# Rows of score maxima by VectorE's 32x32 transposition in place of a TensorE product

## The chip, the cores and the metric

One core of a Trainium2 chip. The metric is the device time of one execution in microseconds (us), taken as the median over runs. Engines: TensorE (PE, with its weight loads as PEld), VectorE (DVE), ScalarE (ACT), GpSimd (POOL) and SyncE (SP), whose queue issues nearly all DMAs here.

## What is computed

Two layers over 2048 tokens of width 1024: a Mamba-2 layer, then a multi-head latent attention. The change lies in the attention, whose core in the reference is

```python
for i in range(S // Q_BLOCK):                  # blocks of 128 queries
    s = einsum('bqhd,bkhd->bhqk', q_nope, k_nope[:, :kv_len]) + \
        einsum('bqhr,bkr->bhqk', q_rope, k_rope[:, :kv_len])
    s = s * scale
    p = softmax(where(mask, s, -inf), axis=-1)
    outs.append(einsum('bhqk,bkhd->bqhd', p, v[:, :kv_len]))
```

with 16 heads, queries and keys of 64 + 32 channels and values of 64. The softmax needs for each query something near its largest score, so that the exponentials stay in range.

## The kernel before

The program runs the Mamba layer and the projections first, then `heads` (the attention), then `back` (gate, output projection, final norm). Only `heads` is touched.

`heads` works on 64 *jobs*, one for each head h (0 to 15) and block qb (0 to 3) of 512 queries. A job has 4 qb + 4 *units*, one for each block kb of 128 keys; the last four are on the causal diagonal. There are 640 units in all, and as many *chunks* of the first pass.

- **First pass, `maxima`** (one chunk of it per step): a product of 128 queries by up to 512 keys in the high half of the fp16 pairs (L1235, on the diagonal with a mask product L1237) into a PSUM tile, and VectorE's maximum over the keys (L1238) into one column of `mx`. After a job's last chunk VectorE makes of `mx` (through `m` and `me`) the 128x8 numbers `nm`: for each of the 128 queries of the job's four groups the negative maximum divided by 64, as an fp16 value (columns 0 to 3, L1249) and its remainder (4 to 7, L1250).
- **`row`**: the numbers of a job must become two rows of 512 queries, since they enter the scores as two more channels: rows 96 and 97 of the query tile `quer[h, qb]`, against constant rows of 64 in the keys. TensorE multiplies `nm` (as weights, 128x128 and zero beyond column 8) by the identity `idb` (L1255), VectorE copies the 8x128 result from PSUM into `rT` (L1257), and SP writes `rT` to DRAM (`m_d`, L1258) and reads it back as 2x512 (L1259). The read waits for the write.
- **Second pass, `scores`** for unit i: three products of 128 keys by 512 queries (L1269 to L1271, the first with 98 channels, that is with the row; L1273 adds the mask on the diagonal), ScalarE's exponential from PSUM (L1275, `x`) and its fp16 copy (L1277, `PTs`), then the remainder `x` - `PTs` by VectorE or, for two in five units off the diagonal, by GpSimd (L1279).
- **`values`**, three units behind: two products for each of up to four query groups (L1291, L1293) into "tr" tiles, and at the end of a half job `finish` (`Ot`, `ri`, `Oa`, `Op`); `store` turns the results of a pair of heads.

TensorE's order is the order in which the code is written (a manual schedule for that engine); on the others the scheduler sets the order. One step of the loop emits at most one or two chunks of maxima, then what is due in `later` (rows, stores), then the scores of unit i, then the values of unit i - 3. All maxima of a job must be out `READY` = 7 units ahead of its first unit; the job's row follows `ROWS` = 2 steps after its last chunk. Where small jobs follow large ones the chunks run further ahead, so a row of qb = 3 is made about 5 units before it is used, rows of the others earlier. Maxima, rows, scores and stores take their PSUM tiles in turn from the four of tag "mm"; a tile is free again when its reader has read it. `rT` and `nm` have two tiles each.

Of the kernel before, what the change touches and what calls it, by code (L numbers as in the profile page):

```python
# [13 lines left out]
F16 = mybir.dt.float16  # L14
# [7 lines left out]
P = 128  # L22
# [5 lines left out]
NH = 16  # L28
EPS = 1e-6
TB = 512  # L30
NB = T // TB
# [8 lines left out]
EV1 = ['big', 'yT', 'Xp', 'big', 'Sp']  # L40
HELD = 3
READY = 7
ROWS = 2
TURN = 4
MSCALE = 64.0
LN16 = 2.772588722239781
# [21 lines left out]
class Net:  # L68
# [716 lines left out]
    def ssd(self, b, g):  # L785
# [30 lines left out]
        for c in range(4):  # L816
# [9 lines left out]
            def between():  # L826
                pi = self.t(self.pp, "tr", [P, TB], bufs=4)
                self.mm3(pi, Ct[:, 0], Ct[:, 1], old[:, 0], old[:, 1], True, True)
                t = self.t(self.sp, "yt", [P, TB], bufs=2)
                v.tensor_tensor(v8(t), v8(pi), heads(ecum), ALU.mult)  # L830
                return t
# [23 lines left out]
            with self.tc.high_priority(20):  # L855
                v.tensor_tensor(v8(Xd), v8(px), heads(dt), ALU.mult)
# [335 lines left out]
    def heads(self, sp):  # L1192
        nc, v, act, mm = self.nc, self.nc.vector, self.nc.scalar.activation, self.nc.tensor.matmul
        keys, vals, quer = self.keys, self.vals, self.quer
        turned = [self.t(sp, f"nm{i}", [P, P], F16, bufs=1) for i in range(2)]
        for u in turned:
            nc.gpsimd.memset(u, 0.0)

# [11 lines left out]
        jobs = [(h, qb) for h in range(NH) for qb in range(NB)]  # L1210
        chunks, ends = [], []
# [14 lines left out]
        def maxima(n, j, i, c0, w, last):  # L1226

            h, qb = jobs[n]
            if (j, i) == (0, 0):
                peak[n] = self.t(sp, "mx", [P, 4, 4], bufs=3)  # L1230
                if n + 2 < len(jobs):
                    self.load_q(*jobs[n + 2])
            Q, K, qs = quer[h, qb], keys[h % 2], slice(j * P, (j + 1) * P)
            s = self.t(self.pp, "mm", [P, TB], bufs=4)
            mm(s[:, :w], Q[0:96, 0, qs], K[0:96, 0, c0:c0 + w], start=True, stop=not last)  # L1235
            if last:
                mm(s[:, w - P:w], self.idb, self.mk, start=False, stop=True)  # L1237
            v.tensor_reduce(peak[n][:, j, i:i + 1], s[:, :w], AX.X, ALU.max)  # L1238
            if last and j == 3:
                m = peak.pop(n)  # L1240
                if qb:
                    x = self.t(sp, "m", [P, 4], bufs=2)
                    v.tensor_reduce(x, m[:, :, :qb + 1], AX.X, ALU.max)
                else:
                    x = m[:, :, 0]
                e = self.t(sp, "me", [P, 4], bufs=2)
                v.tensor_scalar(e, x, -1.0 / MSCALE, LN16 / MSCALE, ALU.mult, ALU.add)
                u = turned[n % 2]
                v.tensor_copy(u[:, 0:4], e)  # L1249
                v.tensor_tensor(u[:, 4:8], e, u[:, 0:4], ALU.subtract)  # L1250

        def row(n):

            ps = self.t(self.pp, "mm", [P, TB], bufs=4)
            mm(ps[:, 0:P], turned[n % 2], self.idb, start=True, stop=True)  # L1255
            r = self.t(sp, "rT", [8, P], F16, bufs=2)
            v.tensor_copy(r, ps[0:8, 0:P])  # L1257
            nc.sync.dma_start(self.m_d[n], r)  # L1258
            nc.sync.dma_start(quer[jobs[n]][96:98, 0, :], self.m_d[n].rearrange("(s j) q -> s (j q)", s=2))  # L1259

        def scores(i):

            n, kb = units[i]
            h, qb = jobs[n]
            jj = max(kb - 4 * qb, 0)
            diag = kb >= 4 * qb
            Q, K, ks, c = quer[h, qb], keys[h % 2], slice(kb * P, (kb + 1) * P), slice(jj * P, TB)
            s = self.t(self.pp, "mm", [P, TB], bufs=4)
            mm(s[:, c], K[0:98, 0, ks], Q[0:98, 0, c], start=True, stop=False)  # L1269
            mm(s[:, c], K[0:96, 0, ks], Q[0:96, 1, c], start=False, stop=False)  # L1270
            mm(s[:, c], K[0:96, 1, ks], Q[0:96, 0, c], start=False, stop=not diag)  # L1271
            if diag:
                mm(s[:, jj * P:(jj + 1) * P], self.mk, self.idb, start=False, stop=True)  # L1273
            x = self.t(sp, "x", [P, TB], bufs=4)
            act(x[:, c], s[:, c], AF.Exp)  # L1275
            u = self.t(sp, "PTs", [P, 2, TB], F16, bufs=HELD + 2)
            act(u[:, 0, c], x[:, c], AF.Copy)  # L1277
            engine = nc.gpsimd if not diag and i % 5 in (1, 3) else v
            engine.tensor_tensor(u[:, 1, c], x[:, c], u[:, 0, c], ALU.subtract)  # L1279
            return u  # L1280

        def values(i, u):

            n, kb = units[i]
            h, qb = jobs[n]
            V = vals[h % 2]
            if kb == 0:
                outs[n] = [self.t(self.pp, "tr", [P, 2, 256], bufs=4) for _ in range(2)]
            for j in range(max(kb - 4 * qb, 0), 4):
                o, js = outs[n][j // 2][:, j % 2], slice(j * P, (j + 1) * P)  # L1290
                mm(o[:, 0:130], u[:, 0, js], V[:, kb, :], start=kb == 0 and j % 2 == 0, stop=False,  # L1291
                   skip_group_check=True)
                mm(o[:, 64:130], u[:, 1, js], V[:, kb, 64:130], start=False, stop=kb == 4 * qb + j,  # L1293
                   skip_group_check=True)
            if kb in (4 * qb + 1, 4 * qb + 3):
                finish(n, (kb - 4 * qb) // 2)
            if kb == 4 * NB - 1 and h + 2 < NH:
                self.load_k(h + 2, 0, NB)
                self.load_v(h + 2)
# [32 lines left out]
        step, later, held, made = [0], [], [], 0  # L1332
# [3 lines left out]
        def waiting():  # L1336
            for at, f in list(later):
                if at <= step[0]:
                    later.remove((at, f))
                    f()  # L1340

        for i in range(len(units)):
            step[0] = i
            while made < due[i]:
                maxima(*chunks[made])
                made += 1
                n = chunks[made - 1][0]
                if made == ends[n]:
                    if i:
                        later.append((i + ROWS, lambda n=n: row(n)))  # L1350
                    else:
                        row(n)
            waiting()
            held.append((i, scores(i)))
            if len(held) > HELD:
                values(*held.pop(0))
# [121 lines left out]
    def run(self):  # L1478
        tc = self.tc
        with ExitStack() as whole:  # L1480
            cp = whole.enter_context(tc.tile_pool(name="const", bufs=1))
            dp = whole.enter_context(tc.tile_pool(name="dram", bufs=1, space=DRAM))
            self.pp = whole.enter_context(tc.tile_pool(name="pp", bufs=4, space=PSUM))
            self.sm = whole.enter_context(tc.tile_pool(name="sm", bufs=4))
            self.constants(cp)
            self.h_d = dp.tile([T, D], F32, name="h_d")
            self.gate_d = dp.tile([D, T], F32, name="gate_d")
            self.o_d = dp.tile([D, T], F32, name="o_d")
            self.m_d = dp.tile([NH * NB, 8, P], F16, name="m_d")
            self.qn_d = dp.tile([1024, 2, T], F16, name="qn_d")  # L1490
            self.q1_d = dp.tile([256, 2, T], F16, name="q1_d")
            self.q2_d = dp.tile([256, 2, T], F16, name="q2_d")
            self.kn_d = dp.tile([1024, 2, T], F16, name="kn_d")
            self.kr_d = dp.tile([32, 2, T], F16, name="kr_d")
            self.v_d = dp.tile([T, 2048], F16, name="v_d")
            self.wd_d = dp.tile([KD, P, 2, 288], F16, name="wd_d")
            self.wq_d = dp.tile([KD, P, 2, 384], F16, name="wq_d")
            self.wg_d = [dp.tile([KD, P, 2, TB], F16, name=f"wg{n}_d") for n in range(2)]
            self.wu_d = [dp.tile([2 if n < 4 else 3, P, 2, TB], F16, name=f"wu{n}_d") for n in range(7)]
            self.us_d = dp.tile([1024], F32, name="us_d")  # L1500
            self.wi_d = [dp.tile([G, KD // 2, P, 2, 2, n], F16, name=f"wi{i}_d") for i, n in enumerate((256, 512, 512))]
            self.wo_d = dp.tile([G, 2, 2, P, 2, 2, TB], F16, name="wo_d")
            self.xq = whole.enter_context(tc.tile_pool(name="xq", bufs=8, side="right"))
            self.layers()
            self.attention()
            self.back()
            self.tail.close()
# [50 lines left out]
```

## Time and profile before

| | |
|---|---|
| median of 3 runs | 3020.39 us (3019.53 to 3021.72) |
| profiled execution | 3012.66 us |
| its span, first to last instruction | 3010.9 us |
| busy in the span | PE 2871.6 us (95%), DVE 2281.5 (76%), ACT 1885.9 (63%), POOL 665.7 (22%) |
| the attention | about 2000 to 2815 us of the span |

The shares are averages over stages: ahead of the attention TensorE alone is full, in the attention TensorE, VectorE and ScalarE are all well used. In the lists, a line reads: time or total, engine, source line, operation, what it writes <- what it reads; a bracket behind an instruction gives how long its engine stood idle before it and what released it. The numbers of matrix products' ends are modelled, so consecutive ones overlap in the list.

### The profile page before, as it was taken

What the parts mean: (1) busy time and instruction counts of PE and PEld (TensorE: products, weight loads), DVE (VectorE), ACT (ScalarE), POOL (GpSimd) and SP (SyncE); (2) the same over time, 40 slices, a digit from 0 to 9 for tenths busy, and PEclk for the clock granted to TensorE, in tenths of its full rate; (3) what the DMA queues carried; (4) which work ended last, traced back from release to release, by engine and by line L of the source; (5) the groups of instructions that cost most, each with busy time, mean ns of one, the idle gap of its engine ahead of it and who ended that gap; (6) DMA issues with size and microseconds to landing.
All of it is one profiled execution on the core that took longest, in us unless ns stands there. A gap on an engine that the chain in (4) does not pass through costs nothing.

```text
span 3010.9 us, 55172 instructions
## 1 busy us (share of the span) xinstructions
PE 2871.6 (95%) x19726; PEld 1686.8 (56%) x19726; DVE 2281.5 (76%) x5162; ACT 1885.9 (63%) x4360; POOL 665.7 (22%) x798
## 2 busy tenths in 40 slices
PE   7899999999999999999999999989999999998998
PEld 3456656555555554544555454545666656665787
DVE  6789987787877788787855544368988989898554
ACT  8777666665766666565543433338888888887622
POOL 0212122121222112221111212113232323234200
PEclk9999999999999999999999999999999999999999
DMA  8765435544464456455357555631212121222462
GB/s 284 241 227 179 155 116 196 175 154 141 168 212 157 145 175 198 172 165 186 123 162 262 176 167 194 201 96 43 62 43 69 43 62 43 69 64 74 141 210 105
DMA packets 234248, 440.70 MB, mean 146 GB/s; under 512 B 59218, under 2 KB 101010, under 8 KB 232532
## 3 DMA queue, kind: packets, MB, share of 16 engines
q1 hardware_dynamic: 222836, 401.24, 41.9%
q0 software_dynamic: 11136, 35.92, 3.3%
q8 instruction: 155, 2.54, 0.3%
q14 instruction: 121, 0.99, 0.1%
HBM read 332.73 MB, written 104.34 MB: 145 GB/s over the span
## 4 chain that ended last, share of the span: by engine, by line
PE 60%; DVE 19%; ACT 10%; issue 6%; DMA 4%; POOL 1%; SPq 0%; ACTq 0%; DVEq 0%; POOLq 0%
PE mm L84 11%; PE mm L86 11%; PE mm L85 11%; PE tr L85 4%; PE tr L84 4%; PE tr L86 4%; DVE cacc L612 4%; ACT x L1275 3%; DVE PTs L1279 3%; DVE mx L1238 3%; ACT PTs L1277 2%; PE mm L1269 2%; PE mm L1270 2%; PE mm L1271 2%; PE tr L1291 2%
## 5 line engine op out<-in xcount | busy, mean ns | idle before, releaser
L1275 ACT ACTIVATE x<-mm 128x512 f32<-128x512 f32 (+3 forms) x640 | 336.1, 525 | 124.9 <-PE mm L1271 59.2
L1238 DVE TENSOR_REDUCE mx<-mm 128x1 f32<-128x512 f32 (+3 forms) x640 | 378.4, 602 | 39.3 <-PE mm L1237 23.4
L1277 ACT ACTIVATE PTs<-x 128x512 f16<-128x512 f32 (+3 forms) x640 | 361.7, 566 | 16.2
L1279 DVE TENSOR_TENSOR PTs<-x,PTs 128x512 f16<-128x512 f32 (+3 forms) x512 | 306.9, 604 | 45.3 <-ACT PTs L1277 35.2
L84 PE MATMUL mm<-xT,wsp 128*128 128x512 f16 x800 | 306.7, 383 | 6.3 <-ACT wsp L115 4.2
L85 PE MATMUL mm<-xT,wsp 128*128 128x512 f16 x800 | 305.7, 382 | 0.0
L86 PE MATMUL mm<-xT,wsp 128*128 128x512 f16 x800 | 305.3, 382 | 0.0
L1291 PE MATMUL tr<-K,PTs 128*128 128x130 f16 x2176 | 280.0, 222 | 0.0
L1293 PE MATMUL tr<-K,PTs 128*128 128x66 f16 x2176 | 260.5, 194 | 9.0 <-POOL PTs L1279 6.2
L1291 PEld LDWEIGHTS <-PTs 128*128 128x128 f16 x2176 | 203.8, 98 | 61.4 <-issue 4.5
L84 PE MATMUL mm<-wsp,xT 128*128 128x512 f16 (+1 forms) x640 | 230.3, 361 | 4.7 <-ACT craw L606 4.5
L85 PE MATMUL mm<-wsp,xT 128*128 128x512 f16 (+1 forms) x640 | 230.5, 360 | 3.2 <-DVE wsp L116 3.2
L612 DVE SCALAR_TENSOR_TENSOR cacc<-craw,pack,cacc 128x512 f32<-128x512 f32 x288 | 214.1, 771 | 24.2 <-ACT cacc L610 23.2
L1269 PE MATMUL mm<-xT,K 98*128 98x512 f16 (+3 forms) x640 | 227.2, 355 | 4.3 <-DVE mx L1238 3.4
L1293 PEld LDWEIGHTS <-PTs 128*128 128x128 f16 x2176 | 197.7, 98 | 59.7 <-POOL PTs L1279 7.9
L86 PE MATMUL mm<-wsp,xT 128*128 128x512 f16 (+1 forms) x640 | 230.5, 360 | 0.0
L1270 PE MATMUL mm<-xT,K 96*128 96x512 f16 (+3 forms) x640 | 227.1, 355 | 0.0
L1235 PE MATMUL mm<-K,xT 96*128 96x512 f16 (+3 forms) x640 | 225.2, 358 | 1.1 <-DVE Xp L116 1.1
L1271 PE MATMUL mm<-xT,K 96*128 96x512 f16 (+3 forms) x640 | 225.6, 352 | 0.0
L802 POOL TENSOR_TENSOR Xp<-Xw,Xp 128x512 fp32r<-128x512 f32 x64 | 89.6, 1400 | 499.6 <-ACT Xp L801 280.5
L84 PE MATMUL mm<-wsp,yT 128*128 128x512 f16 (+1 forms) x512 | 197.5, 386 | 2.2 <-DVE sz L636 1.6
L86 PE MATMUL mm<-wsp,yT 128*128 128x512 f16 (+1 forms) x512 | 195.8, 382 | 0.0
(461 smaller groups left out, 6946.9 us busy)
## 6 DMA issues: line engine op xcount, KB each, us to landing
wsp<-wi_d SPq DMA_DIRECT2D x96, 512.0 KB
big<-cumT SPq DMA_DIRECT2D x64, 512.0 KB
wraw<-in_ssm_w_out_dram SPq DMA_DIRECT2D x96, 256.0 KB
wi_d<-wsp SPq DMA_DIRECT2D x32, 512.0 KB
wsp<-wo_d SPq DMA_DIRECT2D x32, 512.0 KB
wsp<-wu_d SPq DMA_DIRECT2D x28, 512.0 KB
hx<-in_ssm_w_in_dram SPq DMA_DIRECT2D x48, 256.0 KB
wraw<-in_ssm_w_in_dram SPq DMA_DIRECT2D x48, 256.0 KB
```

The costliest lines, as they stand in the source:

```text
L84: mm(out, l_hi, r_hi, start=start, stop=False)
L85: mm(out, l_hi, r_lo, start=False, stop=False)
L86: mm(out, l_lo, r_hi, start=False, stop=stop)
L612: nc.vector.scalar_tensor_tensor(acc, raw[:, k:k + TB], wk[k], acc, ALU.mult, ALU.add)
L1238: v.tensor_reduce(peak[n][:, j, i:i + 1], s[:, :w], AX.X, ALU.max)
L1269: mm(s[:, c], K[0:98, 0, ks], Q[0:98, 0, c], start=True, stop=False)
L1270: mm(s[:, c], K[0:96, 0, ks], Q[0:96, 1, c], start=False, stop=False)
L1275: act(x[:, c], s[:, c], AF.Exp)
L1277: act(u[:, 0, c], x[:, c], AF.Copy)
L1279: engine.tensor_tensor(u[:, 1, c], x[:, c], u[:, 0, c], ALU.subtract)
L1291: mm(o[:, 0:130], u[:, 0, js], V[:, kb, :], start=kb == 0 and j % 2 == 0, stop=False, skip_group_check=True)
L1293: mm(o[:, 64:130], u[:, 1, js], V[:, kb, 64:130], start=False, stop=kb == 4 * qb + j, skip_group_check=True)
```

## The change

The row is no longer made by `row`. At the end of `maxima`, right behind `nm`, VectorE transposes `nm` (now 128x32) in blocks of 32x32 into `rT` (128x32): in each block of 32 partitions the first eight rows then hold the eight numbers of 32 queries. All 128 partitions are written to `m_d`, and two DMAs, one for the values and one for the remainders, collect the sixteen pieces of 32 queries each into a row. `ROWS`, the two steps of delay and the PSUM tile of the product are gone.

```diff
-ROWS = 2
-        turned = [self.t(sp, f"nm{i}", [P, P], F16, bufs=1) for i in range(2)]
+        turned = [self.t(sp, f"nm{i}", [P, 32], F16, bufs=1) for i in range(2)]
...
                 v.tensor_copy(u[:, 0:4], e)
                 v.tensor_tensor(u[:, 4:8], e, u[:, 0:4], ALU.subtract)
-
-        def row(n):
-
-            ps = self.t(self.pp, "mm", [P, TB], bufs=4)
-            mm(ps[:, 0:P], turned[n % 2], self.idb, start=True, stop=True)
-            r = self.t(sp, "rT", [8, P], F16, bufs=2)
-            v.tensor_copy(r, ps[0:8, 0:P])
-            nc.sync.dma_start(self.m_d[n], r)
-            nc.sync.dma_start(quer[jobs[n]][96:98, 0, :], self.m_d[n].rearrange("(s j) q -> s (j q)", s=2))
+                r = self.t(sp, "rT", [P, 32], F16, bufs=2)
+                v.transpose(r, u)
+                nc.sync.dma_start(self.m_d[n], r)
+                rows = self.m_d[n].rearrange("(g r) q -> r g q", r=32)
+                for k in range(2):
+                    nc.sync.dma_start(quer[h, qb][96 + k:97 + k, 0, :].rearrange("p (j g q) -> p j g q", j=4, q=32),
+                                      rows[4 * k:4 * k + 4].unsqueeze(0))
...
-                n = chunks[made - 1][0]
-                if made == ends[n]:
-                    if i:
-                        later.append((i + ROWS, lambda n=n: row(n)))
-                    else:
-                        row(n)
...
-            self.m_d = dp.tile([NH * NB, 8, P], F16, name="m_d")
+            self.m_d = dp.tile([NH * NB, P, 32], F16, name="m_d")
```

How the engines' orders change is shown at the job h = 9, qb = 2. In the names, numbers tell tiles of one tag apart; K and xT are the keys and queries here. TensorE at the step of the row, before:

```order
L1293 MATMUL tr_29877<-K_3813_20590,PTs_30140 128x66
L1235 LDWEIGHTS xT_29746
L1235 MATMUL mm_30232<-K_3814_20591,xT_29746 128x512
L1255 LDWEIGHTS nm_4003_21659
L1255 MATMUL mm_30235<-idb,nm_4003_21659 128x128
L1269 LDWEIGHTS K_3814_20591
L1269 MATMUL mm_30241<-xT_28998,K_3814_20591 128x128
```

and after the change (lines from here on are one to three lower):

```order
L1290 MATMUL tr_29840<-K_3813_20590,PTs_30102 128x66
L1234 LDWEIGHTS xT_29715
L1234 MATMUL mm_30199<-K_3814_20591,xT_29715 128x512
L1266 LDWEIGHTS K_3814_20591
L1266 MATMUL mm_30202<-xT_28970,K_3814_20591 128x128
```

The weight load and product of `nm` are gone between the maxima product and the first scores product; nothing else moves on TensorE. VectorE from the job's `m` on, before:

```order
L1243 TENSOR_REDUCE m_30182<-mx_29933 128x4
L1279 TENSOR_TENSOR PTs_30195<-x_30193,PTs_30195 128x384
L1247 TENSOR_SCALAR me_30184<-m_30182 128x4
L1238 TENSOR_REDUCE mx_30202<-mm_30207 128x1
L1249 CAST nm_4003_21659<-me_30184 128x4
L1279 TENSOR_TENSOR PTs_30217<-x_30215,PTs_30217 128x256
L1250 TENSOR_TENSOR nm_4003_21659<-me_30184,nm_4003_21659 128x4
L1308 RECIPROCAL ri_30224<-tr_29877 128x2
L1310 TENSOR_TENSOR Oa_30226<-tr_29877,Ot_30222 128x128
L1238 TENSOR_REDUCE mx_30202<-mm_30232 128x1
L1257 CAST rT_30237<-mm_30235 8x128
L1279 TENSOR_TENSOR PTs_30248<-x_30246,PTs_30248 128x128
```

and after, from the second write of `nm` on (the rows ahead of it are in the same order):

```order
L1249 TENSOR_TENSOR nm_4003_21659<-me_30146,nm_4003_21659 128x4
L1305 RECIPROCAL ri_30191<-tr_29840 128x2
L1251 STREAM_TRANSPOSE rT_30150<-nm_4003_21659 128x32
L1307 TENSOR_TENSOR Oa_30193<-tr_29840,Ot_30189 128x128
L1237 TENSOR_REDUCE mx_30169<-mm_30199 128x1
L1276 TENSOR_TENSOR PTs_30209<-x_30207,PTs_30209 128x128
```

The cast of `rT` behind the next reduction is replaced by a transposition one instruction behind `nm`, ahead of that reduction. SP's queue at the same job, before:

```order
L1162 DMA K_3813_20590<-kn_d 64x4096
L1163 DMA K_3813_20590<-kr_d 32x4096
L1168 DMA K_3813_20590<-v_d 128x16x128
L1258 DMA m_d<-rT_30237 8x128
L1174 DMA xT_30681<-qn_d 64x2x512
L1175 DMA xT_30681<-q_d 16x2x512
L1176 DMA xT_30681<-q_d 16x2x512
L1259 DMA xT_29645<-m_d 2x512
```

and after:

```order
L1161 DMA K_3813_20590<-kn_d 64x4096
L1162 DMA K_3813_20590<-kr_d 32x4096
L1252 DMA m_d<-rT_30150 128x32
L1167 DMA K_3813_20590<-v_d 128x16x128
L1255 DMA xT_29615<-m_d 1x16x32 x2
L1173 DMA xT_30646<-qn_d 64x2x512
L1174 DMA xT_30646<-q_d 16x2x512
L1175 DMA xT_30646<-q_d 16x2x512
```

The write of `rT` now stands ahead of the load of the next values (`v_d`), and its reads, two for one, ahead of the query loads.

## The prediction

> **What bounds the kernel now.** I read the page's totals first, then the attention's stretch in the view by windows, then the list of who waited for whom there, and last the timeline around single instructions. The change touches the attention alone, which runs from about 2000 to 2815 us of the span.
>
> ```profile
> core 0: us, PE busy (x) PEld busy (x) DVE busy (x) ACT busy (x) POOL busy (x), PEclk, DMA share, GB/s
> 2005.00:2815.00 810.00, 739.88 (x7502) 481.25 (x7503) 723.36 (x1687) 675.98 (x1430) 247.24 (x258) 0.97 0.22 55
> ```
>
> In these 810 us TensorE is idle for 70.1 us and VectorE for 86.6 us: two engines at 91% and 89%, neither full. So each holds the other up in turn, and the waits tell where.
>
> ```profile
> PEld L1255 <- DVE nm L1250: 68.0, 61, 2.5
> ...
> PE mm L1255 <- DVE nm L1250: 54.7, 47, 2.2
> ...
> DVE mx L1238 <- PE mm L1237: 23.4, 46, 1.5
> ...
> PE mm L1269 <- DVE mx L1238: 3.4, 10, 0.6
> ```
>
> Columns: total us, times, longest. Of TensorE's 70.1 us of idleness, 54.7 stand before one product, L1255, which waits for VectorE to finish `nm`. (The 68.0 us of the weight load are the same waits, not a second sum.) This is the product that goes. One head, from its place before the row of job (8,3) to that of (9,3), shows the pattern that repeats; the numbers in brackets are TensorE's idle time and what ended it:
>
> ```profile
> 2437.66 0.23 PE L1255 MATMUL mm<-idb,nm 128*128 128x128 bf16 x1 [0.50 <-DVE nm L1250]
> ...
> 2443.11 0.23 PE L1255 MATMUL mm<-idb,nm 128*128 128x128 bf16 x1 [0.69 <-DVE nm L1250]
> ...
> 2452.50 0.23 PE L1255 MATMUL mm<-idb,nm 128*128 128x128 bf16 x1 [0.39 <-DVE nm L1250]
> 2453.09 0.38 PE L1269 MATMUL mm<-xT,K 98*128 98x512 f16 x1 [0.37 <-DVE mx L1238]
> ...
> 2488.25 0.23 PE L1255 MATMUL mm<-idb,nm 128*128 128x128 bf16 x1
> ```
>
> They belong to qb = 3, 0, 1 and (2488.25) again 3; the one of qb = 2, at 2468.36, follows below. The wait at qb = 3 is 0.50 here and none a head later.
>
> **What the removed wait turns into.** TensorE runs its list in written order, so whatever it no longer waits for at L1255 it may wait for one product later. The four "mm" tiles rotate: maxima product, scores, maxima product, scores. Without the row's tile, scores need the scores' tile of two steps before (ScalarE has read it by then), and a maxima product needs the tile of the maxima product two steps before, so VectorE's reduction L1238 of that one. Here is the dearest case, qb = 2, on TensorE and on VectorE:
>
> ```profile
> 2465.90 0.38 PE L1235 MATMUL mm<-K,xT 96*128 96x512 f16 x1
> ...
> 2468.36 0.23 PE L1255 MATMUL mm<-idb,nm 128*128 128x128 bf16 x1 [2.08 <-DVE nm L1250]
> 2468.43 0.22 PE L1269 MATMUL mm<-xT,K 98*128 98x128 f16 x1
> ...
> 2469.01 0.33 PE L1235 MATMUL mm<-K,xT 96*128 96x384 f16 x1
> ```
>
> ```profile
> 2467.15 0.68 DVE L1238 TENSOR_REDUCE mx<-mm 128x1 f32<-128x512 f32 x1
> ...
> 2468.16 0.15 DVE L1250 TENSOR_TENSOR nm<-me,nm 128x4 f16<-128x4 f32 x1
> ...
> 2470.88 0.42 DVE L1238 TENSOR_REDUCE mx<-mm 128x1 f32<-128x256 f32 x1 [0.61 <-PE mm L1237]
> ...
> 2472.91 0.69 DVE L1238 TENSOR_REDUCE mx<-mm 128x1 f32<-128x512 f32 x1 [0.75 <-PE mm L1235]
> ```
>
> Without L1255, TensorE would do the scores and values (0.58 us from 2468.43 to 2469.01) at once, from about 2466.1, when the product at 2465.90 has had its turn, and stand at the next maxima product at 2466.7. That one needs the reduction which ends at 2467.15 + 0.68 = 2467.83. So it starts at 2467.9 instead of 2469.01: of 2.08 us, 1.1 are won and about 1.2 stand again, one product later. At qb = 3 and 0 the reduction needed is done before TensorE comes, so the whole wait is won; at qb = 1 TensorE comes about 0.1 us before the reduction that ended its 0.37 us.
>
> **The sum.** The product itself takes 0.07 us of TensorE's sequence (2468.36 to the next at 2468.43). Per head, times 16:
> - qb = 3: mean of 0.50 and 0, with 0.07: 0.3, 16 times: 5 us.
> - qb = 0: 0.69 + 0.07 = 0.76: 12 us.
> - qb = 1: 0.39 + 0.37 + 0.07 - 0.1 = 0.7: 11 us.
> - qb = 2: 1.1: 17 us.
>
> The clock adds a term. This head in stretches from row to row (columns as in the first fence: VectorE is the third engine; the third number from the right is TensorE's granted clock), and then the eight microseconds behind the long wait:
>
> ```profile
> 2437.66:2443.11 5.45, 4.76 (x56) 3.32 (x56) 4.83 (x13) 4.50 (x9) 1.16 (x1) 1.00 0.00 1
> 2443.11:2452.50 9.39, 9.00 (x90) 5.54 (x90) 8.57 (x22) 8.10 (x18) 3.56 (x4) 1.00 0.07 23
> 2452.50:2468.36 15.86, 13.41 (x144) 8.93 (x145) 14.39 (x34) 12.43 (x27) 3.03 (x3) 1.00 0.27 62
> 2468.36:2488.25 19.89, 19.83 (x188) 12.83 (x189) 17.51 (x43) 16.76 (x37) 7.24 (x8) 0.91 0.30 64
> ```
>
> ```profile
> 2468.00:2472.00 4.00, 3.64 (x29) 2.31 (x30) 3.25 (x12) 1.87 (x5) 0.76 (x2) 0.73 0.92 152
> 2472.00:2476.00 4.00, 4.00 (x32) 2.22 (x31) 2.78 (x7) 3.39 (x7) 1.20 (x2) 0.84 0.27 63
> ```
>
> The clock is full in three stretches and falls in the last: 0.27 x 4 + 0.16 x 4 = 1.7 us of TensorE lost in this head; over the stage the mean of 0.97 means some 24 us. The waits of 0.4 to 0.7 us are followed by no fall, so a wait cut to 1.2 us should lose less. But VectorE stands behind it: it gets back only its own gaps there (0.61 and 0.75). I take a quarter, 6 us; the ends are 0 and 24.
> On this the Trainium skill ("TensorE: Matmul & The Clock Gate", part 1) says that the clock halves after an idle window of about 3.4 us. The trace differs in this place: the fall comes with a single wait of 2.08 us. By the rule the fall would have another cause and stay; the sum would be 6 us less.
>
> On VectorE a cast from PSUM goes and a transposition of 128x32 comes:
>
> ```profile
> L1257 DVE CAST rT<-mm 8x128 f16<-8x128 f32 x62 | 16.7, 270 | 0.8 <-PE mm L1255 0.8
> ...
> L1250 DVE TENSOR_TENSOR nm<-me,nm 128x4 f16<-128x4 f32 x63 | 10.7, 170 | 1.0
> L1249 DVE CAST nm<-me 128x4 f16<-128x4 f32 x63 | 10.5, 167 | 0.7
> ```
> ```profile
> L1247 DVE TENSOR_SCALAR me<-m x48: 154/848/910, 2004.7 to 2798.7; 128x4 f32<-128x4 f32 x48
> ```
> ```profile
> 2466.50 0.72 POOL L1313 TENSOR_TENSOR Op<-Oa,ri 128x128 f32<-128x128 f32 x1 [7.34 <-DVE m L1243]
> ```
> ```profile
> 2466.87 0.36 DVE L1247 TENSOR_SCALAR me<-m 128x4 f32<-128x4 f32 x1
> ```
>
> The trace has no transposition on VectorE. Nearest are the small casts in SBUF, 0.17 us; for 32 columns instead of 4 I take 0.2. The low end is 0.15. The high end is 0.85, the median of `me` (minimum 0.154), which here ends with GpSimd's instruction: 2467.23 and 2467.22. So VectorE saves 0.07 us a job, 4.5 us in all (ends: saves 8, loses 37). The transposition waits for `nm` just ahead of it on its own engine and for the write of `rT` two jobs back, long landed; behind it stands the next reduction, which TensorE's maxima product two steps on needs, so 0.2 us there reach TensorE where it waits. The smaller memset on GpSimd runs once and is nothing.
>
> The four terms and the clock give 51 us. The check is VectorE, the next bound. In the four stretches quoted for the clock VectorE is busy 45.3 of 50.6 us, so 5.3 us a head is the most that can go without shortening its work; 51 us are 3.2 a head. That would leave it 96% busy, and part of its gaps end on ScalarE, not on TensorE. I take a tenth off: 46 us. The last stretch shows the other side: in it TensorE is full (19.83 of 19.89), so a start won is kept until the next row.
>
> The profiled execution took 3012.66 us (span 3010.9), 7.7 under the median of 3020.39. Against its own time the sum gives 2966.7; on the median, 3020.4 - 46 = 2974.
>
> **What is costed at nothing: the path of the row through memory.** `rT` is written as 128 pieces of 64 bytes instead of 8 of 256, and read by two DMAs of 16 pieces instead of one of 2. This hides behind the seven units' lead. The tightest jobs are qb = 3:
>
> ```profile
> 2437.44 0.16 DVE L1250 TENSOR_TENSOR nm<-me,nm 128x4 f16<-128x4 f32 x1
> ```
> ```profile
> 2438.75 0.28 SPq L1258 DMA_DIRECT2D m_d<-rT  x1
> 2439.94 0.23 SPq L1259 DMA_DIRECT2D xT<-m_d  x1
> ```
> ```profile
> 2443.97 0.38 PE L1269 MATMUL mm<-xT,K 98*128 98x512 f16 x1
> ```
>
> From `nm` (2437.60) to the scores that need the row (2443.97) there are 6.37 us, 5.8 when the 0.57 us of this row are won. The new path: transposition 0.2; write to read 1.19 plus the price of more pieces; a second issue 0.23; landing. One head's keys and values load in 2464 to 2472, where 16 DMA engines are 92% busy, with 2048 pieces of 256 bytes among it, 128 an engine: at most 7.4/128 = 0.06 us a piece, so 8 pieces an engine add at most 0.5. Landing: in job (2,3) the read was issued late and the scores still did not wait:
>
> ```profile
> 2464.00:2472.00 8.00, 5.92 (x55) 3.80 (x53) 7.19 (x24) 4.79 (x13) 1.47 (x3) 0.86 0.92 184
> ```
> ```profile
> 2141.27 0.23 SPq L1259 DMA_DIRECT2D xT<-m_d  x1
> ```
> ```profile
> 2143.24 0.38 PE L1269 MATMUL mm<-xT,K 98*128 98x512 f16 x1
> ```
>
> So at most 1.97. Together 0.2 + 1.7 + 0.5 + 2.0 = 4.4 of 5.8 us. On SP's queue the second read stands ahead of query loads for jobs to come and of the output's stores, and costs them 0.23 us; the write also moves ahead of the value load at a head's end, which only helps it. If this cover goes, the late one is the scores product at L1269.
>
> **The rivals.**
> - *All of it comes back as tile waits.* For: half of qb = 2 does in the working above, and after it VectorE is short of nothing but time. Then remain VectorE's 4.5 us, the products' 64 x 0.07 = 4.5 and qb = 3's part of 5: 14 us, 3006. Against: at qb = 0, 1 and 3 the reductions are done early.
> - *Everything is won.* 54.7 + 4.5 + 3.4 of tile waits at L1269 and half of the clock's 24: 74 us, 2946. Against: VectorE would have to be full.
> - *The clock stays as it is.* 40 us: 2980.
> - *The transposition is held up by GpSimd as `me` is.* At 0.85 us VectorE gets 37 us more instead of 4.5 less; most of the 46 is gone: 3010. It turns slower from 0.27 + 46/64 = 1.0 us each.
> - *Slower: the row comes late.* Sixteen rows (qb = 3) have 5.8 us. At a path of 8.7 us the 16 x 2.9 us eat the 46; with 10 us it loses 16 x 4.2 - 46 = 21: 3041. For that, write to read must grow from 1.19 to about 7 us. Nothing in the rows prices 64-byte pieces that high.
> The Trainium skill ("DMA: Bandwidth & Descriptors", specifications) says that transfers under 512 bytes turn into read-modify-writes and miss the full rate; the change goes from 256 and 1024 bytes to 64. By that rule the path is dearer than before, which is this rival; no row here shows 64 bytes.
>
> That the change doesn't do what it says is excluded by the order of the instructions: the product is out of TensorE's list, the transposition in VectorE's.
>
> **How the numbers follow.** Chances: the forecast 0.46, clock stays 0.14, all comes back 0.18, everything won 0.12, transposition held up 0.05, row late 0.05. Predicted: 2974. The likeliest case's own range is 2962 to 2988. For 8 in 10 it must reach towards 3006 and 2946: 2950 to 3004, which leaves out about half of the two gains' ends and the last two rivals. A measurement tells 0.2%, 6 us. Faster: the first four and most of the held-up transposition, 0.92; same 0.04; slower 0.04.
>
> **What would show it.** Right: no L1255; a transposition of 0.2 us, 64 times; TensorE's idle time in the attention near 30 us, now before maxima products (waiting for `mx`), the longest near 1.2 us at qb = 2; a granted clock above 0.97 there; VectorE 94% or more busy; no wait of the scores for a DMA. It is wrong if the waits before the maxima products come near 55 us, if transpositions last as long as `me`, or if scores wait for `m_d`.

## The result, and the profile after

The changed kernel takes 2967.46 us (2962.79 to 2969.3) against 3019.96: ratio 0.9823, 95% interval 0.9806 to 0.984, 52 us less. In a second comparison, with eleven runs of the kernel before at a median of 3015.17, it took 2966.71: 0.9838 (0.9823 to 0.9854), 48 us less. One of the six runs of the changed kernel there took 10438.53 us; the median counts it, the ratio does not. The forecast was 2974, with a range of 2950 to 3004. The profiled execution took 2967.12 (span 2965.3), 45.5 us less than that of before.

All of it lies in the attention, which now ends 45 us earlier: the last product of the values starts at 2777.4 instead of 2822.9. In the view by windows (columns as before):

```profile
2005.00:2770.00 765.00, 728.57 (x7441) 475.69 (x7440) 700.94 (x1683) 675.05 (x1431) 239.98 (x259) 0.98 0.22 58
```

TensorE's idle time there went from 70.1 to 36.4 us, and its busy time from 739.9 to 728.6: some 4.5 for the 64 products; the rest fits the clock, whose mean rose from 0.97 to 0.98. TensorE's part of the list of waits, after:

```profile
PE mm L1266 <- ACT x L1272: 14.7, 48, 0.5
...
PE mm L1266 <- DVE mx L1237: 6.0, 12, 1.2
...
PE tr L1290 <- POOL PTs L1276: 5.6, 3, 3.2
...
PE mm L1266 <- DMA xT<-m_d: 4.2, 5, 1.1
```

The 54.7 us of waiting for `nm` are gone. In their place the first scores product (now L1266) waits 48 times for ScalarE's exponential (14.7 us, against 0.6 before), 12 times for a reduction (6.0, against 3.4), and, new, five times for the row itself. The transposition in the list of groups:

```profile
L1251 DVE STREAM_TRANSPOSE rT<-nm 128x32 f16<-128x32 f16 x63 | 13.0, 206 | 0.3
```

The mean is 0.206 us, and all 64 (one lies ahead of this window) last between 0.197 and 0.214, while the `me` of the same trace last between 0.152 and 0.908. The one at 2035.07 takes 0.21 us although a GpSimd instruction runs from 2034.90 to 2036.06: it is not held up as `me` is. VectorE's idle time fell from 86.6 to 64.1 us, 92% busy.

The job of qb = 2 in head 9, for which the prediction worked out where the wait goes, now reads on TensorE, VectorE and ScalarE:

```profile
2438.76 0.33 PE L1234 MATMUL mm<-K,xT 96*128 96x384 f16 x1
2439.39 0.38 PE L1266 MATMUL mm<-xT,K 98*128 98x512 f16 x1 [0.30 <-ACT x L1272]
```
```profile
2439.22 0.68 DVE L1237 TENSOR_REDUCE mx<-mm 128x1 f32<-128x512 f32 x1
```
```profile
2438.34 0.37 ACT L1272 ACTIVATE x<-mm 128x256 f32<-128x256 f32 x1
...
2439.06 0.28 ACT L1272 ACTIVATE x<-mm 128x128 f32<-128x128 f32 x1
```

The maxima product at 2438.76 is the one that was to wait for the reduction of two steps before. It starts before that reduction even begins (2439.22). So it stands in another tile. The exponential of 2438.34 ends at 2438.71, just ahead of it, so this is most likely the tile of those scores. Contrary to the description of the kernel before, the four tiles of tag "mm" are thus not handed out strictly in turn. The price comes one product later: the scores start when the exponential at 2439.06 has ended (2439.34), 0.30 us late, and so for a few more steps.

### The profile page after: what moved, and what is told of

Its sections match the earlier page's. It is cut to its first block, busy times and chain, and to the rows that moved or that the text cites. A ratio compares the mean times of both kernels' runs of the same rounds, so it can differ in the third digit from the quotient of the medians.

```text
span 2965.3 us, 55123 instructions
## 1 busy us (share of the span) xinstructions
PE 2862.1 (97%) x19662; PEld 1680.9 (57%) x19662; DVE 2258.8 (76%) x5162; ACT 1885.2 (64%) x4360; POOL 653.6 (22%) x798
## 4 chain that ended last, share of the span: by engine, by line
PE 37%; ACT 5%; DVE 5%; issue 3%; DMA 1%; POOL 1%; SPq 0%; DVEq 0%; POOLq 0%; ACTq 0%
PE mm L83 4%; PE mm L84 4%; PE mm L85 4%; PE tr L83 3%; PE mm L1266 3%; PE tr L85 3%; PE tr L84 3%; ACT x L1272 3%; PE mm L1267 3%; PE mm L1268 3%; PE tr L1288 2%; PE mm L1234 2%; ACT PTs L1274 2%; PE tr L1290 1%; DVE mx L1237 1%
## 5 line engine op out<-in xcount | busy, mean ns | idle before, releaser
L1266 PE MATMUL mm<-xT,K 98*128 98x512 f16 (+3 forms) x640 | 224.7, 351 | 26.3 <-ACT x L1272 14.7
```

## The experiments

Differences from the kernel before are to its median in the same comparison: 3016.64 for the first four runs, 3015.17 for the filled wait and for the attempt at the end, 3016.15 for the other four. The changed kernel itself ran only beside the 3015.17, 48 us less, and in the comparison of the result; differences from it are to these two medians, 2967.46 and 2966.71.

**The product later instead of removed.** The kernel before with

```diff
-ROWS = 2
+ROWS = 3
```

> The kernel before, with its product and cast kept, but the row three steps behind the last chunk instead of two. Theory (what cost was TensorE's in-order wait for nm, and the clock's falls behind the longest of them): a step is about 1.25 us, so the waits of 0.4 to 0.7 us at qb = 0, 1 and 3 go and those of 2.08 us shrink to about 0.8; some 40 of the 54.7 us of waits and the eight falls of the clock (1.55 us each, 12 us) go, the product (4.5 us) stays: 2975 to 2988. Rival 1 (the product, its PSUM tile and the cast are the cost): same as before, 3015 to 3022. Rival 2 (the row is late then): scores wait for it, 16 jobs by 1 us or so, 2995 to 3005.

2988.27 us, ratio 0.9911 (0.9894 to 0.9927): 28 us less, just past the upper end of what the theory expected.

```profile
PE mm L1255 <- DVE nm L1250: 24.7, 18, 2.4
PE mm L1269 <- DVE mx L1238: 14.2, 30, 1.8
```

More than half of the gain comes with product, PSUM tile and cast all in place; the first rival falls. The waits for `nm` shrank by 30 us, of which 11 came back as waits for a reduction and 4.5 as waits for ScalarE (0.6 before, 5.1 here). Those at qb = 2 shrank to 1.34 us each, not to the 0.8 expected.

**The wait put back.** The changed kernel (`nm` again 128x128, the transposition reads its first 32 columns) with

```diff
+        def extra(n):
+            ps = self.t(self.pp, "mm", [P, TB], bufs=4)
+            mm(ps[:, 0:P], turned[n % 2], self.idb, start=True, stop=True)
...
+                n = chunks[made - 1][0]
+                if made == ends[n] and i:
+                    later.append((i + 2, lambda n=n: extra(n)))
```

> The changed kernel with the product of nm and the identity put back on TensorE at its old place, two steps behind the last chunk; nobody reads its result, the row still comes from the transposition. Theory (the wait is the cost): 40 us or more come back, 3008 to 3020, with TensorE's waits for nm near 50 us and the clock's falls back. Rival (the gain came from the row being made earlier, or from the cast leaving VectorE): 2970 to 2980.

3019.13 us, ratio 1.0007 (0.9998 to 1.0017): all of the gain is gone, though the row is made as in the changed kernel, without the cast.

```profile
PE mm L1261 <- DVE nm L1249: 51.7, 45, 3.0
```

This line covers the span up to 2770 us; over the whole attention it is 54.6 us in 48 waits.

**The product without the wait.** The same with `self.idb` in place of `turned[n % 2]` (`nm` stays 128x32 here):

> As the kernel with the wait put back, but the product takes the constant identity on both sides, so that it waits for nothing but its PSUM tile; nobody reads it. It prices the product and its tile without the wait. Theory: 62 x 0.07 = 4.5 us and a little for the tile: 2970 to 2978. Rival (the fourth user of the four tiles is what hurt): over 2990.

2975.45 us, ratio 0.987 (0.9855 to 0.9885): 8 us more than the changed kernel. So product and tile are about 8, and the waiting, with what follows from it, some 44: that is the difference between the two last runs, 3019.13 and 2975.45.

**More work on VectorE.** The changed kernel with

```diff
                 v.transpose(r, u)
+                v.transpose(self.t(sp, "rX", [P, 32], F16, bufs=2), u)
```

> The changed kernel with a second transposition of nm into a scratch tile behind the first: 64 x 0.21 = 13 us more on VectorE, nothing else. Theory (VectorE is the next bound, 92% busy in the attention): half of it or more shows, 2974 to 2982. Rival (VectorE's time is hidden, TensorE alone sets the pace): no change, 2964 to 2970.

2970.68 us, ratio 0.9854 (0.9839 to 0.9869). The second transposition lasts 0.169 us, 10.8 us in all; The time is 3 to 4 us above the changed kernel's two medians, but the intervals overlap, so this is not clear of noise. It lies just above the rival's range and below the theory's: of VectorE's time at this place about a third counts at most, and perhaps nothing.

**The wait at qb = 2 alone, and at the others alone.** The kernel with the wait put back, with

```diff
-                if made == ends[n] and i:
+                if made == ends[n] and i and jobs[n][1] == 2:
```

> The changed kernel with the unread product of nm put back only in the sixteen jobs of qb = 2, where the wait before was 2.08 us. It sizes that term. By the prediction (half of the wait would have come back anyway one product later, and a quarter of the clock's loss): 17 + 6 = 23 us, 2990. By what the trace after shows (the maxima product behind it does not wait at all, and no fall of the clock is left in the steady heads): 16 x 2.1 less some 0.4 of later waits, and eight falls by 1.55, 35 to 45 us: 3002 to 3012.

2990.32 us, ratio 0.9918 (0.9895 to 0.9941). And with `!= 2`:

> The same with the product put back only in the jobs of qb = 0, 1 and 3 (46 of them). By the prediction 5 + 12 + 11 = 28 us: 2995. By the shift of the scores between the two traces, head by head, about 0.5 + 0.65 + 0.55 = 1.7 us a head and no clock: 25 us, 2988 to 2996. If this and the one with qb = 2 together give much more or less than 52 us, the waits are not independent.

2993.67 us, ratio 0.9928 (0.991 to 0.9946). Against the changed kernel they cost 23 and 26 us, 49 together, products and tiles included: the whole gain within the noise, so the two add up. The first figure is the prediction's 23, not the 35 to 45 that I read from the trace after. What I had left out is in its list of waits:

```profile
PE mm L1261 <- DVE nm L1249: 32.7, 16, 2.2
PE mm L1271 <- DMA xT<-m_d: 5.0, 4, 2.5
PE mm L1271 <- DVE mx L1237: 4.8, 11, 0.5
...
PE mm L1271 <- ACT x L1277: 0.4, 1, 0.4
```

With the wait of 2.08 us at qb = 2 in place, the 14.7 us of waits for ScalarE are gone (0.4). These are the returned half: not one wait of 1.2 us, but some three of 0.3 in the steps behind. With only the other waits put back they stay:

```profile
PE mm L1261 <- DVE nm L1249: 21.4, 32, 1.8
PE mm L1271 <- ACT x L1277: 14.7, 48, 0.5
```

**The clock apart from the wait.** To the kernel with the wait at qb = 2 alone, 24 products that wait for nothing, ahead of the waiting one:

```diff
+            for _ in range(24):
+                mm(ps[:, 0:P], self.idb, self.idb, start=True, stop=True)
             mm(ps[:, 0:P], turned[n % 2], self.idb, start=True, stop=True)
```

> The kernel with the wait put back at qb = 2 alone, and 24 unread products of the identity by itself (some 1.35 us) ahead of the waiting one: they fill the wait of 2.08 us, so that TensorE is idle for about 0.7 us instead, and TensorE's later work starts as late as without them. It separates the clock's falls from the wait. If the falls cost time of their own (1.55 us by the heads of the kernel before with and without one, some 6 heads): no fall left in the steady heads, 2978 to 2984. If VectorE hides them: 2988 to 2992, as without the filling. If the fall has nothing to do with this wait, falls remain.

2980.24 us, ratio 0.9886 (0.9871 to 0.9902): 10 us faster with 384 products more. TensorE's timeline there:

```profile
2446.24 0.38 PE L1234 MATMUL mm<-K,xT 96*128 96x512 f16 x1
2446.46 1.50 PE L1262 MATMUL mm<-idb 128*128 128x128 bf16 x24
2448.70 0.23 PE L1263 MATMUL mm<-idb,nm 128*128 128x128 bf16 x1 [0.74 <-DVE nm L1249]
```

The steady heads (2025 to 2650 us) in the view by windows, the granted clock third from the right; first before and after, then the wait at qb = 2, and the same filled:

```profile
2025.00:2650.00 625.00, 576.64 (x5898) 376.14 (x5896) 563.72 (x1334) 526.33 (x1116) 182.99 (x199) 0.98 0.22 53
```
```profile
2025.00:2650.00 625.00, 601.69 (x6252) 395.26 (x6250) 584.18 (x1420) 561.97 (x1192) 190.45 (x213) 1.00 0.23 59
```
```profile
2025.00:2650.00 625.00, 590.56 (x6134) 390.39 (x6133) 581.04 (x1393) 545.36 (x1165) 197.89 (x208) 0.99 0.22 56
```
```profile
2025.00:2650.00 625.00, 607.76 (x6525) 408.28 (x6523) 588.17 (x1409) 550.96 (x1181) 196.69 (x209) 1.00 0.23 57
```

In windows of 2 us these stretches show eight falls of the clock behind twelve waits of 2.08 us or a little more before the change, none after it, five behind thirteen with the wait at qb = 2, and none with the wait filled. Each fall takes some 1.7 us of full clock away. Summed over 2000 to 2830 us the lost clock is 25.0 us before, 14.7 after, 26.6 with the wait and 15.3 with it filled.

With the idle time cut to 0.74 us the clock stays full: the falls come from this wait. They cost about 10 us of the 23 (the four runs of the two kernels do not overlap: 2986.50 to 2992.89 against 2978.59 to 2982.00), which fits the 11 us of lost clock between them. The other 13 are the waiting, with the product and its tile in these sixteen jobs.

**The path through memory.** The changed kernel, where the write puts the pieces in their places and one DMA reads two rows:

```diff
-                nc.sync.dma_start(self.m_d[n], r)
-                rows = self.m_d[n].rearrange("(g r) q -> r g q", r=32)
-                for k in range(2):
-                    nc.sync.dma_start(quer[h, qb][96 + k:97 + k, 0, :].rearrange("p (j g q) -> p j g q", j=4, q=32),
-                                      rows[4 * k:4 * k + 4].unsqueeze(0))
+                nc.sync.dma_start(self.m_d[n].rearrange("r (g q) -> g r q", q=32), r)
+                nc.sync.dma_start(quer[h, qb][96:98, 0, :], self.m_d[n][0:8].rearrange("(s j) q -> s (j q)", s=2))
```

> The changed kernel with the sixteen pieces put in place by the write instead of the reads: the write goes to 32 rows of 128 numbers, and one DMA reads two rows of 512 as before the change. SP issues one DMA of 0.23 us instead of two that last 1.38 us together, so the row comes 1.1 us earlier. Theory (the five waits of the scores for the row, 4.2 us, are what is left of the path through memory): 2961 to 2965, none of those waits left. Rival (those waits only moved other waits): no change, 2966 to 2969.

2967.19 us, ratio 0.984 (0.9822 to 0.9857): no change. The waits for the row went from 4.2 to 1.5 us, too little to be told from none.

```profile
PE mm L1263 <- DMA xT<-m_d: 1.5, 2, 1.2
```

**The row too late.** The kernel before with `ROWS = 4`:

> The kernel before with its product four steps behind the last chunk. With three steps it took 2988, with 24.7 us of waits for nm left. Theory: the waits for nm go, the product's 8 us stay, as with the product that waits for nothing (2975), if the row is still in time; only three steps (3.8 us) are left for cast, write and read, about 3.5 us in the 16 jobs of qb = 3, so some of them wait: 2974 to 2986. Rival (TensorE waits elsewhere for VectorE as it did at three steps, 14.2 us for mx): 2985 to 2995.

3027.2 us, ratio 1.0038 (1.0024 to 1.0053), slower than before and outside what either expected.

```profile
PE mm L1269 <- DMA xT<-m_d: 33.0, 15, 2.8
...
PE mm L1255 <- ACT x L1275: 3.6, 14, 0.3
```

The waits for `nm` are gone, as forecast, but in 15 jobs the scores wait 2.2 us each for the row (up to 2790 us of the span; 34.2 us in 16 waits over the whole attention), and the clock falls behind these waits too (mean 0.97 in the steady heads). This is the wait of the prediction's slower rival, the late row, seen in another kernel: three steps are too short for cast, write and read.

**An attempt at a better version.** The kernel with one read, and GpSimd takes some remainders on the diagonal:

```diff
-            engine = nc.gpsimd if not diag and i % 5 in (1, 3) else v
+            engine = nc.gpsimd if not jj and i % 5 in (1, 3) else v
```

> An attempt at a better version: the kernel with one read, and GpSimd also takes the remainder of the first diagonal unit (512 wide) of a job in two cases of five: some 26 x 0.69 = 18 us off VectorE. If VectorE is on the path as the second transposition showed (13 us more of VectorE cost some 3 us): 2961 to 2965. Rival (GpSimd's 1.17 us come too late for the values, or hold up VectorE's small instructions): 2967 or more.

2966.6 us, ratio 0.9839 (0.9823 to 0.9855), beside the changed kernel in the same comparison:

> The changed kernel unchanged, for comparison with the attempt on the same chip: 2965 to 2969, the same by either theory.

2966.71 us, 0.9838. No gain, although VectorE is busy for 10 us less than in the kernel with one read (696.5 against 706.5 us from 2005 to 2770): no sign of VectorE's time on the path here. No version was found that beats the changed kernel.

## Why the prediction was right, point by point

- *The bound and the mechanism* (TensorE's wait for `nm` in its written order): shown. The wait put back takes the whole gain away, the product without it only 8 us.
- *The sum*, 46 us: 45.5 between the two profiled executions, 48 to 52 between medians. So the runs can't tell the 46 from the 51 that stood there before a tenth was taken off for VectorE, and the tenth is not shown. The spread of the kernel before (3009 to 3022 over all comparisons) is wider than the gap between these figures.
- *qb = 3, 0 and 1*: 28 us forecast, 26 measured for the three together; they were not taken apart.
- *qb = 2*: 17 + 6 forecast, 23 measured in all, but 13 of waiting and 10 of clock. That the total fits is luck: one term was 4 us too large, the other 4 too small. That about half comes back was right in kind; the place was wrong. The premise that a maxima product needs the tile of two steps before failed (2438.76 against 2439.22), and the waits returned on the scores, for ScalarE: 14.7 us, 0.9 of each 2.08 instead of the 1.2 forecast.
- *The clock*: the quarter was too little. The ground for it, that VectorE stands behind the clock and gives back only its gaps, did not hold for this wait: the filling won about 10 us. By the idle window of about 3.4 us in the Trainium skill ("TensorE: Matmul & The Clock Gate", part 1) the falls would have stayed; the runs differ: they went when a wait of 2.1 us went, and came back with it.
- *The product itself*: 4.5 us forecast, 8 measured with its tile. What the other 3.5 are was not taken apart; the trace of that run shows 3.8 us of waits of the product for its tile.
- *The transposition*: 0.2 forecast, 0.206 measured; held up by GpSimd: no.
- *VectorE 94% busy*: 92%. Its time was less of a bound than I took it for: 10.8 us more of it cost 4 at most against those medians, and 10 less won nothing.
- *The signs*: `L1255` is gone, the transpositions and the clock (0.98) are as named. TensorE's idle time is 36.4 us, not 30, and most of it stands before the scores, only 0.2 before maxima products. And one sign of being wrong came true: the scores waited for `m_d`, five times.
- *The path of the row costs nothing*: off by 4.2 us of waits. From transposition to landing I had 4.4 us, and the path where it was late is

```profile
2035.31 0.32 SPq L1252 DMA_DIRECT2D m_d<-rT  x1
2036.76 1.38 SPq L1255 DMA_DIRECT2D xT<-m_d  x2
```
```profile
2039.45 0.38 PE L1266 MATMUL mm<-xT,K 98*128 98x512 f16 x1 [1.14 <-DMA xT<-m_d]
```

from the end of the transposition at 2035.28 to 2039.45, 4.2 us. That this comes near to 4.4 is partly luck. The two reads hold SP for 1.38 us, where the sum has 0.46, and land 1.3 us behind that, where it has at most 1.74 (1.97 less an issue of 0.23). The sum is also off as written: 1.19 + 0.23 is 1.42, not 1.7, so it should give 4.1. In heads 5 and 12 the read was issued 2.9 and 2.5 us behind the write instead of 1.4, and the path took 6.0 and 5.4 us; what kept the read there is open. What was wrong above all is the time there is. I took 5.8 us from `nm` on, but the scores were due 3.0 us after the transposition in this job (head 0), and 4.2 to 5.1 at qb = 3 in heads 1 to 15, so hardly anything was left to spare. Repairing it won nothing that can be measured.

## What to carry to other kernels

On an engine that runs a list in written order, look for the one instruction that waits for another engine's latest result, and price it by its wait, not by its duration: here 64 products of 0.07 us stood for 54.7 us of waiting, and without the waits some 44 us were won, clock included. Then follow what the engine does next, since a part of the wait returns at the following buffers (14.7 us here), and look at what an idle stretch does to the clock. Delaying the instruction is the cheaper first try, and it has a cliff: one step later won 28 us, two steps later lost 11.

## What the runs showed of the hardware

The granted clock fell behind single idle stretches of 2.1 us in some of the steady heads (8 of 12 before, 5 of 13 with the wait at qb = 2), behind one of twelve of 1.34 us (with `ROWS = 3`), and behind none of 0.74 us; filling the idle stretch with unread products won 10 us. One DMA that fills a part of one SBUF row from 16 pieces of 64 bytes holds SP for 0.65 us, one of two pieces of 1 KB for 0.23, the write of 128 pieces of 64 bytes for 0.325, and the same write scattered over rows for 0.55. So neither bytes nor the number of pieces alone sets the time of an issue: the 16 pieces of 1 KB in all cost twice the 128 pieces of 8 KB.
